# A set's chunks in two goes beside U, and gate weights made one item ahead behind it

## The chip, the cores and the metric

The kernel runs on one core of one Trainium2 chip. The metric is the device time of one execution in microseconds (us); the runs shown are given as a median with the lowest and the highest. A profile is one further execution, recorded instruction by instruction. The engines are PE (matrix multiply; PEld is its loading of stationary operands), DVE (vector), ACT (scalar, activation functions), POOL (here nearly only gathers, that is, indirect DMAs) and SP (which issues plain DMAs). Each runs its own queue in order, and they wait for one another by semaphores.

## What is computed

One layer of a diffusion backbone on 256 latent tokens with 256 context tokens: modulated norm, a combined projection, an mLSTM and a differential attention, gates and an output projection, and then PEER, a retrieval of single-neuron experts. The change lies in PEER and in what follows it. All is float32.

```python
def peer(h, w_pq, sub_keys, expert_u, expert_v):
    ...
    def block(args):
        hx, ix, gx = args
        act = jax.nn.gelu(jnp.einsum('td,ted->te', hx, expert_u[ix]).astype(jnp.float32), approximate=False)
        return jnp.einsum('te,ted->td', (gx * act).astype(h.dtype), expert_v[ix])
...
x = x + g2 * peer(modulate(rmsnorm(x, norm2_w[l]), sh2, sc2), w_pq[l], sub_keys[l], expert_u[l], expert_v[l])
return rmsnorm(x, final_norm_w)
```

Per token and head, ix holds the best 16 of 128 x 128 experts and gx their softmax weights. There are 16384 experts of 2048 numbers in expert_u and in expert_v; each of the 256 tokens takes 128 of them.

## The kernel before

**U.** The kernel computes the product of every token with every row of expert_u. The experts come in 128 columns of 128. A column takes two half blocks of 512 KB: SP loads one (`raw`), ACT casts its high part (`hi`), DVE subtracts to get the low part (`lo`), and PE multiplies both against the tokens (8 matmuls with hi, 8 with lo, tile `s`). Three buffers each of raw, hi and lo let the load run ahead. `u_pair` does two columns; behind each half block `pump` takes steps of the generator `plan`, 1.3 of them on average in the last stretch, so that other work is put between half blocks. GELU goes to `act` and from there to DRAM (`ag_dram`), beside the gates g.

**V.** The output is the sum over experts of gate x activation x row of expert_v. Lists made on the chip say which rows are needed by which 32 tokens. V works on blocks of 128 rows. POOL gathers per block the two factors (`ag`, from ag_dram) and the rows (`vraw`, 1 MB); DVE multiplies the two factors into the block's weights `w`. There are four sorts of blocks. A *set* is four blocks, one for each group of 32 tokens of one 128-token tile; its weights are 32 wide and PE multiplies them with the rows as they are, in four chunks of 512 columns (`v_groups`). `PAIRS` are four blocks that serve a group of 32 in both tiles, in the same manner. *BOTH* and *single* blocks have weights for all 128 tokens of both tiles or of one; here rows and weights are each cut into a high and a low part (`split`: hi and lo, three buffers; `halves`: ACT casts l0, DVE subtracts to l1), and PE makes three products of them, in groups of six matmuls for a half of the columns and one tile (`v_part`). Two *dense* blocks, the last two columns (`N_LIST` = 126 and up), take their weights from `act_tail`, for all 256 tokens at once, into `d`, which has one buffer (`weights_of`, L1571 to L1574).

**Order.** `SOON` are seven sets that `soon()` does beside U, as steps of `plan`. Those of the first tile add up in PSUM (`out_acc[0]`, matmuls that write `v`). The second tile's accumulators are not yet there, so its two sets write each chunk into one of two PSUM buffers `vs`, and ACT copies it (first set, L1670) or DVE adds it (second set, L1668) into `kept`. `multiply` puts all four chunks in one step. Behind U, `out_acc[1]` starts from `kept`, and `ITEMS` follow in order: two sets of the second tile, the two dense blocks, then four rounds of BOTH, single, BOTH, single and so on with a `PAIRS` item in each, and at the end three sets: one of the first tile, two of the second. `v_item(n)` calls `next_item(n)`, which first issues gathers (`fetch`, up to a dozen blocks ahead; twelve rows and twelve `ag` fit), then makes the weights of item n, and then PE's matmuls of item n follow. On DVE the operations marked `line` keep the order in which they are written; PE's and POOL's keep theirs too. ACT's casts and DVE's lo are placed by the scheduler.

**End.** `residual(t, c)` (L1790) multiplies chunk c of a tile with g2 and adds x1 on DVE, and squares it on ACT; `finish_tile(t)` (L1799) sums the squares, takes the root on POOL, scales the four chunks and sends them out. Before the change the order is: set of the first tile; its four residuals; weights and matmuls of the last set but one; weights of the last set; `finish_tile(0)`; the last set's matmuls chunk by chunk, each with its residual; `finish_tile(1)`.

Of the kernel before, what the change touches and what calls it, by code (L numbers as in the profile page):

```python
# [31 lines left out]
P = 128  # L32
D = 2048
T = 256
# [53 lines left out]
def build(tc, a, dump=None):  # L88
# [1475 lines left out]
    def halves(src, n, name, bufs, pool=None):  # L1564
        pool = pool or vst
        r = [pool.tile([P, n], F32R, name=f"{name}{s}", tag=f"{name}{s}", bufs=bufs) for s in range(2)]
        nc.scalar.copy(r[0], src)
        line(nc.vector.tensor_tensor(r[1], src, r[0].bitcast(F32), op=OP.subtract))  # L1568
        return r

    def weights_of(kind, ins):  # L1571
        if kind == DENSE:
            r = halves(act_tail[:, ins - N_LIST, :], T, "d", 1)
            return {t: [x[:, t * P:(t + 1) * P] for x in r] for t in range(2)}  # L1574
        out = {}
        for t, ag in ins.items():
            if kind < 8 or kind >= PAIR:
                g = slice(32 * (group(kind, t) % 2), 32 * (group(kind, t) % 2) + 32)
                out[t] = vst.tile([P, 32], F32, name="w32", tag="w32", bufs=16)
                line(nc.vector.tensor_tensor(out[t], ag[:, 0, 0, g], ag[:, 0, 1, g], op=OP.mult))  # L1580
                continue
            w = vst.tile([P, P], F32, name="w", tag="w", bufs=2)
            line(nc.vector.tensor_tensor(w.rearrange("p (q c) -> p q c", q=2), ag[:, :, 0], ag[:, :, 1], op=OP.mult))  # L1583
            out[t] = halves(w, P, "l", 5)
        return out
# [16 lines left out]
            fetched.append((stage_rows(*BLOCKS_OF[b]), ins))  # L1602
            staged[0] += 1

    def next_item(n):
        fetch(n)
        return [(raw, weights_of(kind, ins)) for (kind, _), (raw, ins) in
                zip(ITEMS[n], [fetched.pop(0) for _ in ITEMS[n]])]

    def accumulators(t):  # L1610
        pool = tc.alloc_tile_pool(name=f"psV{t}", bufs=1, space=PSUM, side=("left", "right")[t], reuse_waits="tile")
# [40 lines left out]
    def soon():  # L1652
        nonlocal psG
        loads = resident()
        psG.release()
        out_acc[0] = accumulators(0)
        work = SOON + ITEMS[:2]
        sums = [0, 0]

        def multiply(item, parts):  # L1660
            t = item[0][0] // 4
            if t == 0:
                v_groups(0, item, parts, first=not sums[0])
            for c in range(4 * t):
                ps = psS.tile([P, 512], F32, name="vs", tag="vs")
                v_groups(1, item, parts, (c,), first=True, last=True, into=ps)
                if sums[1]:
                    line(nc.vector.tensor_tensor(kept[c], ps, kept[c], op=OP.add))  # L1668
                else:
                    nc.scalar.copy(kept[c], ps)  # L1670
            sums[t] += 1

        for n, item in enumerate(work):
            new = []
            if n == 0:
                rows = []
                for b in work[0] + work[1]:
                    rows.append(stage_rows(*b))
                    yield
            for b in item:  # L1680
                while made[0] < columns_of(*b):
                    yield
                new.append(stage_gates(*b))
                yield
            if 0 < n <= len(SOON):
                parts = [(raw, weights_of(kind, ins)) for (kind, _), (raw, ins) in zip(work[n - 1], held)]
            for j, b in enumerate(item):
                new[j] = (stage_rows(*b) if n > 1 else rows.pop(0)), new[j]
                next(loads, None)
                yield  # L1690
            if 0 < n <= len(SOON):
                multiply(work[n - 1], parts)
                yield
            held = new
            if n >= len(SOON):
                fetched.extend(new)
                staged[0] += len(new)
# [3 lines left out]
    for i1 in range(0, P, 2):  # L1701
# [3 lines left out]
        act = act_tail if i1 == N_LIST else gm.tile([P, 2, T], F32, name="act", tag="act", bufs=2)  # L1705
        u_pair(act, pace)
        if i1 == N_LIST:
            parts = next_item(0)
        nc.scalar.activation(act, act, AF.Gelu)
        if i1 < N_LIST:  # L1710
            rows = ag_dram[P + i1 * P:P + (i1 + 2) * P].rearrange("(i p) (t c) -> p i t c", p=P, t=2)
# [22 lines left out]
                v_part(hl, ins[t], t, hf_)  # L1734

    def v_item(n):
        parts = next_item(n)
        if len(parts) > 1:
            for t in parts[0][1]:
                v_groups(t, ITEMS[n], parts)  # L1740
        else:
            v_block(*parts[0])

    for c in range(4):
        mp_(out_acc[1][c], lhsT=ident, rhs=kept[c], start=True, stop=False, skip_group_check=True)
    v_groups(1, ITEMS[0], parts)
    x1[1] = [chunk("x1", "o2") for _ in range(3)] + [kept[3]]
    for c in range(4):
# [66 lines left out]
    fw = [stg.tile([P, 1024], F32, name="fw", tag="raw", bufs=3) for _ in range(2)]  # L1815
    for i in range(2):
        nc.sync.dma_start(fw[i], bass.AP(tensor=fnw.tensor, offset=fnw.offset + i * 1024, ap=[[0, P], [1, 1024]]))
    v_groups(0, ITEMS[N_LAST], next_item(N_LAST), last=True)
    for c in range(4):
        residual(0, c)  # L1820
    last = next_item(N_LAST + 1)
    v_groups(1, ITEMS[N_LAST + 1], last)
    last = next_item(N_LAST + 2)
    finish_tile(0)
    for c in range(4):
        v_groups(1, ITEMS[N_LAST + 2], last, (c,), last=True)
        residual(1, c)
# [72 lines left out]
```

## Time and profile before

| | us |
|---|---|
| median of 3 runs | 2257.23 (2255.82 to 2258.28) |
| profiled execution, its time | 2255.45 |
| profiled execution, its span | 2253.7 |
| PE busy in the span | 2153.0 |
| DVE, ACT, POOL busy | 1533.7, 1021.8, 789.2 |
| last eight matmuls of U start / first set behind U starts | 2025.5 / 2030.2 |
| last set's matmuls end (as modelled) | 2239.0 |

The span is what the trace covers; the time is 1.75 us more. In a row of a timeline the columns are start, length, engine, line, operation, output<-inputs, count, and in brackets the idle time of the engine just before and what ended it. Names are those of the program without buffer numbers: `w` there stands for w and for the 32 wide w32, `l` for l0 and l1, `d` for d0 and d1. A matmul on float32 operands shows as two records, so the 16 matmuls of a set are 32 records. A line can be that of a helper: nearly all matmuls stand at L94, so one reads by tiles.

### The profile page before, as it was taken

How to read it: one execution, taken by the hardware profiler on the slowest of the kernel's cores; microseconds unless marked ns; L12 is line 12 of the kernel's file. 1: busy time of each engine (PE TensorE's matmuls, PEld its weight loads, DVE VectorE, ACT ScalarE, POOL GpSimd, SP SyncE). 2: the span in 40 equal slices, each digit the busy share in tenths (PEclk: the TensorE clock that was granted, in tenths of full speed). 3: DMA queues.
4: the chain of work that ended last, by engine and by line, in shares of the span. 5: the costliest groups of instructions: out<-in, count | busy, mean ns of one | idle time of the engine just before them, and what ended most of it. 6: DMA issues, size and time to landing. Idle time of an engine off the chain costs nothing. (4 is left out here: it accounts for less than half of the span.)

```text
span 2253.7 us, 37192 instructions
## 1 busy us (share of the span) xinstructions
PE 2153.0 (96%) x14098; PEld 1863.2 (83%) x14098; DVE 1533.7 (68%) x2779; ACT 1021.8 (45%) x1632; POOL 789.2 (35%) x799
## 2 busy tenths in 40 slices
PE   6999999999999999998999999998999899999996
PEld 3668998999899999987998888897888776785663
DVE  3438793676986786855679967777999444444655
ACT  3232232224565844444444768873445343333442
POOL 2122210235464320000224657761221423316664
PEclk9999999999999999999999999999999999999998
DMA  9958882776555578875556658888665889989996
GB/s 380 370 172 304 320 295 90 281 254 200 169 160 149 167 266 275 279 254 192 169 169 192 191 172 236 225 225 251 203 196 181 338 311 339 349 286 409 392 357 234
DMA packets 235845, 563.63 MB, mean 250 GB/s; under 512 B 85218, under 2 KB 118803, under 8 KB 222096
## 3 DMA queue, kind: packets, MB, share of 16 engines
q1 hardware_dynamic: 155328, 339.34, 45.8%
q0 software_dynamic: 45488, 204.33, 25.2%
q10 hardware_dynamic: 34848, 17.57, 2.7%
q8 instruction: 111, 1.82, 0.3%
q14 instruction: 70, 0.57, 0.1%
HBM read 516.99 MB, written 38.93 MB: 247 GB/s over the span
## 5 line engine op out<-in xcount | busy, mean ns | idle before, releaser
L140 ACT CAST hi<-raw 128x1024 fp32r<-128x1024 f32 x528 | 553.1, 1049 | 857.5 <-PE acc L300 266.4
L143 DVE TENSOR_TENSOR lo<-raw,hi 128x1024 fp32r<-128x1024 f32 x476 | 599.8, 1263 | 377.7 <-ACT hi L140 341.6
L94 PE MATMUL s<-h,hi 128*128 128x512 f32 x2048 | 528.9, 400 | 13.1 <-ACT hi L140 11.9
L94 PEld LDWEIGHTS s<-h,hi 128*128 128x128 f32 x2048 | 369.9, 190 | 90.9 <-ACT hi L140 16.7
L300 PE MATMUL acc<-hL,hi 128*128 128x256 f32 x2048 | 334.0, 285 | 0.0
L94 PEld LDWEIGHTS s<-h,lo 128*128 128x128 f32 x2048 | 279.4, 190 | 29.7 <-DVE lo L143 5.6
L300 PEld LDWEIGHTS acc<-hL,hi 128*128 128x128 f32 x2048 | 293.3, 192 | 1.8 <-ACT kA L677 0.3
L94 PE MATMUL s<-h,lo 128*128 128x256 f32 x2048 | 286.1, 282 | 6.7 <-DVE lo L143 3.9
L143 POOL TENSOR_TENSOR lo<-raw,hi 128x1024 fp32r<-128x1024 f32 x52 | 133.7, 2572 | 306.9 <-ACT hi L140 243.7
L300 PE MATMUL acc<-hL,lo 128*128 128x256 f32 x1024 | 176.3, 285 | 0.8 <-DVE lo L143 0.8
L533 DVE SCALAR_TENSOR_TENSOR raw<-raw,cr 128x1024 f32<-128x1024 f32 x128 | 155.2, 1227 | 23.6 <-DMA raw<-w_mod 20.2
L118 POOL DMA_DIRECT2D raw<-w_mod x128 | 67.9, 530 | 291.5 <-DVE raw L533 278.0
L1261 POOL TENSOR_SCALAR o<-iota,i1T,gT 128x128 f32<-128x128 f32 x128 | 145.1, 1142 | 58.6 <-PE g L94 29.0
L1532 POOL DMA_INDIRECT vraw<-expert_v,idxV x96 | 101.7, 1060 | 175.5 <-PE v L94 94.2
L300 PEld LDWEIGHTS acc<-hL,lo 128*128 128x128 f32 x1024 | 150.8, 192 | 2.0 <-DVE lo L143 1.0
L1532 POOL DMA_INDIRECT ag<-ag_dram,idxG x96 | 115.6, 1204 | 83.0 <-DMA ag_dram<-act 43.0
L1561 DVE TENSOR_TENSOR lo<-vraw,hi 128x1024 fp32r<-128x1024 f32 x68 | 82.8, 1223 | 83.5 <-ACT hi L1559 82.8
L1244 DVE TENSOR_REDUCE act<-s 128x256 f32<-128x512 f32 x126 | 86.2, 684 | 56.9 <-PE s L94 53.4
L300 PE MATMUL acc<-hC,hi 128*128 128x256 f32 x512 | 124.7, 283 | 0.0
L94 PE MATMUL v<-hi,l 128*128 128x512 f32 x384 | 108.5, 399 | 4.8 <-DVE l L1568 4.6
L1559 ACT CAST hi<-vraw 128x1024 fp32r<-128x1024 f32 x68 | 70.7, 1049 | 91.2 <-PE v L94 89.3
L300 PEld LDWEIGHTS acc<-hC,hi 128*128 128x128 f32 x512 | 98.3, 192 | 0.0
(444 smaller groups left out, 3330.7 us busy)
## 6 DMA issues: line engine op xcount, KB each, us to landing
raw<-expert_u SPq DMA_DIRECT2D x256, 512.0 KB, 4.2
raw<-w_in SPq DMA_DIRECT2D x176, 512.0 KB, 4.5
raw<-w_mod POOLq DMA_DIRECT2D x128, 512.0 KB, 5.3
raw<-w_mod SPq DMA_DIRECT2D x64, 512.0 KB, 8.3
raw<-w_out SPq DMA_DIRECT2D x32, 512.0 KB, 4.3
raw<-w_pq SPq DMA_DIRECT2D x32, 512.0 KB, 3.4
ag_dram<-gates SPq DMA_DIRECT2D x32, 512.0 KB, 6.2
ag_dram<-act ACTq DMA_DIRECT2D x126, 128.0 KB, 4.5
```

The lines of the kernel that those rows point to most:

```text
L94: tc.keep_in_program_order(mm(*args, **kw))
L118: d = queue.dma_start(r, src)
L140: nc.scalar.copy(h, r)
L143: (nc.vector if shared[0] else nc.gpsimd).tensor_tensor(l, r, h.bitcast(F32), op=OP.subtract)
L300: mm(acc[c][:, g * T:(g + 1) * T], lhsT=hl[sb][:, k2 * 512 + c * P:k2 * 512 + (c + 1) * P], rhs=rhs(sa, g, k), start=first and k2 == 0 and ...
L533: product = nc.vector.scalar_tensor_tensor(r, r, 1.0, cr, op0=OP.mult, op1=OP.mult, accum_out=part[:, h, i:i + 1])
L1244: line(nc.vector.reduce_sum(act[:, e], ps.rearrange("p s t -> p t s"), axis=AX.X))
L1261: (nc.gpsimd if i % 2 else nc.vector).tensor_scalar(o2[:, i], iota, cols[:, i:i + 1], factor[:, i:i + 1], op0=OP.is_equal, op1=OP.mult)
L1532: tc.keep_in_program_order(nc.gpsimd.indirect_dma_start(out=out, out_offset=None, in_=src, in_offset=bass.IndirectOffsetOnAxis(ap=idx[:, b ...
L1559: nc.scalar.copy(h, raw)
L1561: nc.vector.tensor_tensor(l, raw, h.bitcast(F32), op=OP.subtract)
```

## The change

It has four parts. `multiply` gives two extra steps behind chunk 1 of a set of the second tile, so that half blocks of U come between its two halves. A dense block's weights are made for each tile apart, in the tag `l` with five buffers in place of `d` with one. `next_item` is split into `fetch` and `item_weights`; behind U, `v_item(n)` fetches, takes the weights made before, and makes those of item n + 1 ahead of its own matmuls. At the end, the weights of the last set but one are made ahead of the first tile's last matmuls, and those of the last set behind that tile's second residual.

```diff
@@ -1570,8 +1570,7 @@
 
     def weights_of(kind, ins):
         if kind == DENSE:
-            r = halves(act_tail[:, ins - N_LIST, :], T, "d", 1)
-            return {t: [x[:, t * P:(t + 1) * P] for x in r] for t in range(2)}
+            return {t: halves(act_tail[:, ins - N_LIST, t * P:(t + 1) * P], P, "l", 5) for t in range(2)}
         out = {}
         for t, ag in ins.items():
             if kind < 8 or kind >= PAIR:
@@ -1602,10 +1601,11 @@
             fetched.append((stage_rows(*BLOCKS_OF[b]), ins))
             staged[0] += 1
 
-    def next_item(n):
-        fetch(n)
+    def item_weights(n):
         return [(raw, weights_of(kind, ins)) for (kind, _), (raw, ins) in
                 zip(ITEMS[n], [fetched.pop(0) for _ in ITEMS[n]])]
+
+    coming = []
 
     def accumulators(t):
         pool = tc.alloc_tile_pool(name=f"psV{t}", bufs=1, space=PSUM, side=("left", "right")[t], reuse_waits="tile")
@@ -1668,7 +1668,11 @@
                     line(nc.vector.tensor_tensor(kept[c], ps, kept[c], op=OP.add))
                 else:
                     nc.scalar.copy(kept[c], ps)
+                if c == 1:
+                    yield
+                    yield
             sums[t] += 1
+            yield
 
         for n, item in enumerate(work):
             new = []
@@ -1689,8 +1693,7 @@
                 next(loads, None)
                 yield
             if 0 < n <= len(SOON):
-                multiply(work[n - 1], parts)
-                yield
+                yield from multiply(work[n - 1], parts)
             held = new
             if n >= len(SOON):
                 fetched.extend(new)
@@ -1705,7 +1708,8 @@
         act = act_tail if i1 == N_LIST else gm.tile([P, 2, T], F32, name="act", tag="act", bufs=2)
         u_pair(act, pace)
         if i1 == N_LIST:
-            parts = next_item(0)
+            fetch(0)
+            parts = item_weights(0)
         nc.scalar.activation(act, act, AF.Gelu)
         if i1 < N_LIST:
             rows = ag_dram[P + i1 * P:P + (i1 + 2) * P].rearrange("(i p) (t c) -> p i t c", p=P, t=2)
@@ -1734,7 +1738,9 @@
                 v_part(hl, ins[t], t, hf_)
 
     def v_item(n):
-        parts = next_item(n)
+        fetch(n)
+        parts = coming.pop()
+        coming.append(item_weights(n + 1))
         if len(parts) > 1:
             for t in parts[0][1]:
                 v_groups(t, ITEMS[n], parts)
@@ -1743,6 +1749,7 @@
 
     for c in range(4):
         mp_(out_acc[1][c], lhsT=ident, rhs=kept[c], start=True, stop=False, skip_group_check=True)
+    coming.append(item_weights(1))
     v_groups(1, ITEMS[0], parts)
     x1[1] = [chunk("x1", "o2") for _ in range(3)] + [kept[3]]
     for c in range(4):
@@ -1815,13 +1822,17 @@
     fw = [stg.tile([P, 1024], F32, name="fw", tag="raw", bufs=3) for _ in range(2)]
     for i in range(2):
         nc.sync.dma_start(fw[i], bass.AP(tensor=fnw.tensor, offset=fnw.offset + i * 1024, ap=[[0, P], [1, 1024]]))
-    v_groups(0, ITEMS[N_LAST], next_item(N_LAST), last=True)
-    for c in range(4):
+    fetch(N_LAST)
+    coming.append(item_weights(N_LAST + 1))
+    v_groups(0, ITEMS[N_LAST], coming.pop(0), last=True)
+    for c in range(2):
         residual(0, c)
-    last = next_item(N_LAST + 1)
-    v_groups(1, ITEMS[N_LAST + 1], last)
-    last = next_item(N_LAST + 2)
+    coming.append(item_weights(N_LAST + 2))
+    for c in range(2, 4):
+        residual(0, c)
+    v_groups(1, ITEMS[N_LAST + 1], coming.pop(0))
     finish_tile(0)
+    last = coming.pop()
     for c in range(4):
         v_groups(1, ITEMS[N_LAST + 2], last, (c,), last=True)
         residual(1, c)
```

On PE, in the second of the two sets beside U. Before, its chunks 1 and 2 (two `vs` buffers, the same four weights):

```order
L94 MATMUL vs_19572<-vraw_19280,w32_19478 32x512
L94 MATMUL vs_19572<-vraw_19280,w32_19480 32x512
L94 MATMUL vs_19572<-vraw_19305,w32_19482 32x512
L94 MATMUL vs_19572<-vraw_19305,w32_19484 32x512
L94 MATMUL vs_19578<-vraw_19280,w32_19478 32x512
L94 MATMUL vs_19578<-vraw_19280,w32_19480 32x512
L94 MATMUL vs_19578<-vraw_19305,w32_19482 32x512
L94 MATMUL vs_19578<-vraw_19305,w32_19484 32x512
```

and after the change, from chunk 1 of the same set on:

```order
L94 MATMUL vs_19594<-vraw_19302,w32_19502 32x512
L94 MATMUL vs_19594<-vraw_19302,w32_19504 32x512
L94 MATMUL vs_19594<-vraw_19355,w32_19506 32x512
L94 MATMUL vs_19594<-vraw_19355,w32_19508 32x512
L94 MATMUL s_19601<-h2_0_10160,hi_19543 128x512
L94 MATMUL s_19601<-h2_1_10161,hi_19543 128x512
L94 MATMUL s_19601<-h2_2_10162,hi_19543 128x512
L94 MATMUL s_19601<-h2_3_10163,hi_19543 128x512
```

Two half blocks of U (32 matmuls) now stand between chunks 1 and 2; the set as a whole comes one half block later in U.

On DVE, in the rounds behind U, around a BOTH block (rows vraw_21519 before, vraw_21543 after) and the single that follows it. Before:

```order
L1583 TENSOR_TENSOR w_21817<-ag_21517 128x128
L1561 TENSOR_TENSOR lo_21831<-vraw_21519,hi_21829 128x1024
L1568 TENSOR_TENSOR l1_21820<-w_21817,l0_21819 128x128
L1583 TENSOR_TENSOR w_21823<-ag_21517 128x128
L1561 TENSOR_TENSOR lo_21847<-vraw_21519,hi_21845 128x1024
L1583 TENSOR_TENSOR w_21861<-ag_21521 128x128
L1561 TENSOR_TENSOR lo_21869<-vraw_21519,hi_21867 128x1024
L1568 TENSOR_TENSOR l1_21826<-w_21823,l0_21825 128x128
L1568 TENSOR_TENSOR l1_21864<-w_21861,l0_21863 128x128
L1561 TENSOR_TENSOR lo_21879<-vraw_21519,hi_21877 128x1024
```

and after:

```order
L1582 TENSOR_TENSOR w_21798<-ag_21541 128x128
L1561 TENSOR_TENSOR lo_21812<-vraw_21462,hi_21810 128x1024
L1568 TENSOR_TENSOR l1_21801<-w_21798,l0_21800 128x128
L1582 TENSOR_TENSOR w_21804<-ag_21541 128x128
L1561 TENSOR_TENSOR lo_21822<-vraw_21462,hi_21820 128x1024
L1582 TENSOR_TENSOR w_21837<-ag_21545 128x128
L1568 TENSOR_TENSOR l1_21807<-w_21804,l0_21806 128x128
L1561 TENSOR_TENSOR lo_21845<-vraw_21543,hi_21843 128x1024
L1568 TENSOR_TENSOR l1_21840<-w_21837,l0_21839 128x128
L1561 TENSOR_TENSOR lo_21861<-vraw_21543,hi_21859 128x1024
```

Before, the low weights of the block's second tile (l1_21826) stand behind three of the lo of the block and the single; after, they (l1_21807) stand ahead of the block's first lo, behind those of the single before it.

On DVE at the end: yf and x are the first tile's residuals, the w32 the weights of the last sets. Before, from the first tile's third residual on:

```order
L1793 TENSOR_TENSOR yf_22520<-v02_18449,g2_2_18910 128x512
L1794 TENSOR_TENSOR x1_18693<-x1_18693,yf_22520 128x512
L1793 TENSOR_TENSOR yf_22524<-v03_18450,g2_3_18912 128x512
L1794 TENSOR_TENSOR x1m_18687<-x1m_18687,yf_22524 128x512
L1580 TENSOR_TENSOR w32_22528<-ag_22312 128x32
L1580 TENSOR_TENSOR w32_22530<-ag_22316 128x32
L1580 TENSOR_TENSOR w32_22532<-ag_22319 128x32
L1580 TENSOR_TENSOR w32_22534<-ag_22323 128x32
L1580 TENSOR_TENSOR w32_22552<-ag_22396 128x32
L1580 TENSOR_TENSOR w32_22554<-ag_22400 128x32
L1580 TENSOR_TENSOR w32_22556<-ag_22481 128x32
L1580 TENSOR_TENSOR w32_22558<-ag_22485 128x32
```

and after, from its second residual on:

```order
L1800 TENSOR_TENSOR yf_22532<-v01_18448,g2_1_18884 128x512
L1801 TENSOR_TENSOR x1_18692<-x1_18692,yf_22532 128x512
L1579 TENSOR_TENSOR w32_22536<-ag_22416 128x32
L1579 TENSOR_TENSOR w32_22538<-ag_22420 128x32
L1579 TENSOR_TENSOR w32_22540<-ag_22497 128x32
L1579 TENSOR_TENSOR w32_22542<-ag_22501 128x32
L1800 TENSOR_TENSOR yf_22544<-v02_18449,g2_2_18910 128x512
L1801 TENSOR_TENSOR x1_18693<-x1_18693,yf_22544 128x512
L1800 TENSOR_TENSOR yf_22548<-v03_18450,g2_3_18912 128x512
L1801 TENSOR_TENSOR x1m_18687<-x1m_18687,yf_22548 128x512
```

The last set's four weights now stand ahead of the first tile's third and fourth residuals; those of the set before it stand ahead of the first residual. The order of POOL's gathers and of SP's loads is the same in both programs.

## The prediction

> **What bounds the kernel now.** I read the page first, then the busy time by stretch, the waits, and last the timelines of the places that the change touches.
>
> ```profile
> PE 2153.0 (96%) x14098; PEld 1863.2 (83%) x14098; DVE 1533.7 (68%) x2779; ACT 1021.8 (45%) x1632; POOL 789.2 (35%) x799
> ```
>
> The matmul queue (PE) is busy for 96% of the span, so a gain can only come from PE's pauses, from matmuls that run slowly, or from the few microseconds behind the last matmul. The change touches nothing before 1840 us. By stretch:
>
> ```profile
> 1840.00:2026.00 186.00, 178.40 (x1065) 140.36 (x1064) 86.83 (x105) 65.40 (x70) 48.80 (x45) 0.98 0.88 325
> 2026.00:2206.00 180.00, 173.70 (x887) 115.12 (x885) 99.72 (x197) 76.98 (x111) 118.39 (x104) 0.99 0.96 380
> 2040.00:2110.00 70.00, 66.34 (x305) 47.37 (x304) 38.90 (x76) 30.34 (x44) 49.55 (x45) 0.98 1.02 412
> ```
>
> Columns are the stretch, its length, busy time of PE, weight loads, DVE, ACT, POOL, granted clock, DMA share, GB/s. PE lacks 7.6 us of 186 while U still runs, and 6.3 us of 180 behind it. DVE, ACT and POOL have room on average, so a PE pause is a matter of order, not of load. The transfers are another thing: 412 GB/s at a share of 1.02 for 70 us is all they do anywhere. The waits of PE from 1700 us on (total, times, longest):
>
> ```profile
> PE s L94 <- ACT hi L140: 7.5, 6, 3.5
> PE v L94 <- DVE l L1568: 4.6, 11, 0.7
> PE vs L94 <- DVE kept L1668: 4.5, 1, 4.5
> ```
>
> The first is U waiting for its own input; the change only moves when that can happen. The other two are pauses that it goes for.
>
> **Part 1: the second tile's sets beside U in two goes.** PE's timeline around both sets (start, length, idle before and its releaser):
>
> ```profile
> 1844.53 1.92 PE L94 MATMUL vs<-vraw,w 128*32 128x512 f32 x16
> 1847.27 1.06 PE L94 MATMUL vs<-vraw,w 128*32 128x512 f32 x8 [0.82 <-ACT kept L1670]
> 1849.56 1.06 PE L94 MATMUL vs<-vraw,w 128*32 128x512 f32 x8 [1.23 <-ACT kept L1670]
> 1850.56 2.11 PE L94 MATMUL s<-h,hi 128*128 128x512 f32 x8
> ...
> 1870.31 3.64 PE L94 MATMUL v<-vraw,w 128*32 128x512 f32 x32
> 1873.88 2.14 PE L94 MATMUL s<-h,hi 128*128 128x512 f32 x8
> ...
> 1876.79 2.00 PE L94 MATMUL s<-h,hi 128*128 128x512 f32 x8
> ...
> 1893.64 1.92 PE L94 MATMUL vs<-vraw,w 128*32 128x512 f32 x16
> 1900.10 3.64 PE L94 MATMUL vs<-vraw,w 128*32 128x512 f32 x16 [4.54 <-DVE kept L1668]
> 1903.67 3.01 PE L94 MATMUL s<-h,hi 128*128 128x512 f32 x8
> ...
> 1907.46 2.00 PE L94 MATMUL s<-h,hi 128*128 128x512 f32 x8
> ```
>
> A set of the first tile, which waits for nothing, takes 1873.88 - 1870.31 = 3.57 us, and a half block of U behind it 1876.79 - 1873.88 = 2.91. The first of the two sets takes 1850.56 - 1844.53 = 6.03, so 2.46 too much. The second with its half block takes 1907.46 - 1893.64 = 13.82 against 3.57 + 2.91 = 6.48, so 7.34 too much: 4.54 of waiting, and slow matmuls behind it (16 in 3.64 where 1.92 do, 8 in 3.01 where 2.14 do). With two half blocks of U between the goes, the two copies (ACT) or additions (DVE) that chunks 2 and 3 wait for have some 5.8 us. Both stalls go: 9.8. What is late next is U's input, because the pause had covered it:
>
> ```profile
> 1893.23 1.05 ACT L140 CAST hi<-raw 128x1024 fp32r<-128x1024 f32 x1 [4.41 <-DMA raw<-expert_u]
> ```
>
> This half is ready at 1894.28, and the second set now comes one half block later, so PE wants it at 1893.64 and waits 0.6. I take 9.2. The lower end is one wait of the longest kind above (3.5) on top: 5.7; the upper 9.8. The four more steps (1.3 per half block) push the loads of the last early set some three half blocks back; POOL's gathers then rest until U ends, so that costs nothing:
>
> ```profile
> 2024.11 0.95 POOL L1532 DMA_INDIRECT ag<-ag_dram,idxG  x1 [43.02 <-DMA ag_dram<-act]
> ```
>
> **Part 2: dense weights in five buffers.** Behind U, PE multiplies two dense blocks, in eight groups of six:
>
> ```profile
> 2040.09 1.09 PE L94 MATMUL v<-hi,d 128*128 128x512 f32 x4
> ...
> 2041.49 1.09 PE L94 MATMUL v<-hi,d 128*128 128x512 f32 x4
> ...
> 2044.23 0.73 PE L94 MATMUL v<-hi,d 128*128 128x512 f32 x2 [1.18 <-ACT d L1567]
> 2045.72 1.22 PE L94 MATMUL v<-hi,d 128*128 128x512 f32 x2 [0.76 <-DVE d L1568]
> ...
> 2052.74 1.17 PE L94 MATMUL v<-hi,l 128*128 128x512 f32 x4
> ```
>
> A group takes 2041.49 - 2040.09 = 1.40. The last five should take 7.0 and take 2052.74 - 2041.49 = 11.25: 4.25 lost, because the one buffer d makes the second block's weights wait for the first block's matmuls. With the weights of both blocks made at U's end this goes, but for some 0.3 at the step to the first listed block, where no d is waited for: 3.9. The four smaller casts and subtractions replace two larger ones while PE still multiplies the sets in front. Lower end: the waiting alone, 1.18 + 0.76 = 1.9. The other 2.3 are matmuls at about half pace (1.22 for two, where two take 0.62 in part 3's rows). The Trainium skill, "TensorE: Matmul & The Clock Gate" (Part 1: The HAM clock gate, the "warmup" mystery), lets the clock drop only after an idle window of about 3.4 us; by that rule these pauses would cost no clock and the sum would be 2.0 smaller, but in this trace pauses of 1.18 and 0.76 did bring slow matmuls, and the measurement decides.
>
> **Part 3: weights one item ahead.** Of the eleven waits for l, one:
>
> ```profile
> 2146.74 1.09 PE L94 MATMUL v<-hi,l 128*128 128x512 f32 x4
> ...
> 2148.14 0.62 PE L94 MATMUL v<-hi,l 128*128 128x512 f32 x2
> 2149.16 0.73 PE L94 MATMUL v<-hi,l 128*128 128x512 f32 x2 [0.40 <-DVE l L1568]
> ...
> 2150.20 1.09 PE L94 MATMUL v<-hi,l 128*128 128x512 f32 x4
> ```
>
> A group takes 2148.14 - 2146.74 = 1.40, this one 2150.20 - 2148.14 = 2.06: 0.66 lost. The order shows why: DVE makes the second tile's low weights two lo behind their w. Now they stand ahead of the block's own first lo, and w, cast and l of an item are all queued while PE still multiplies the one before. The same DVE and ACT work is done, only sooner. The queue that it moves past holds hi and lo; DVE is busy 99.72 of 180 us there, so a lo that starts two short operations later stays ahead of PE. Ten of the eleven come before 2206 us: 10 x 0.66, and 0.3 for the longest (0.7): 6.9. If the low weights come only half as much sooner, 3.4. PE's gain moves the time at which the buffers of the last group of four come free.
>
> **Part 4: the last weights nearer the front.** From there on POOL's gathers set the pace:
>
> ```profile
> 2206.29 0.94 POOL L1532 DMA_INDIRECT vraw<-expert_v,idxV  x1 [5.72 <-PE v L94]
> ...
> 2224.86 0.94 POOL L1532 DMA_INDIRECT ag<-ag_dram,idxG  x1 [0.31 <-issue]
> ```
>
> ```profile
> 2216.85 0.73 PE L94 MATMUL v<-hi,l 128*128 128x512 f32 x2 [0.39 <-DVE l L1568]
> 2230.35 8.67 PE L94 MATMUL v<-vraw,w 128*32 128x512 f32 x64 [3.13 <-DVE w L1580]
> ```
>
> ```profile
> 2227.46 0.68 DVE L1793 TENSOR_TENSOR yf<-v,g 128x512 f32<-128x512 f32 x1
> ...
> 2229.51 0.69 DVE L1794 TENSOR_TENSOR x1m<-x1m,yf 128x512 f32<-128x512 f32 x1
> ...
> 2231.18 0.19 DVE L1580 TENSOR_TENSOR w<-ag 128x32 f32<-128x32 f32 x1 [0.27 <-DMA ag<-ag_dram,idxG]
> 2231.29 0.15 DVE L1800 TENSOR_REDUCE s<-s 128x1 f32<-128x4 f32 x1
> ...
> 2234.33 0.74 DVE L1809 SCALAR_TENSOR_TENSOR x<-x,rf,fw 128x512 f32<-128x512 f32 x1
> 2236.49 0.69 DVE L1793 TENSOR_TENSOR yf<-v,g 128x512 f32<-128x512 f32 x1 [1.42 <-PE v L94]
> ```
>
> PE's pause of 3.13 goes, but the end does not come sooner. POOL starts this chain when the last group of four is done and then waits for nothing, so the last gates land at the same distance from that point: 2231.18 on the old clock. DVE now asks for them after two residuals instead of four. Queued behind that wait are residuals 2 and 3 of the first tile, its sum, its four scalings, and all of the second tile's end. So the third residual starts at 2231.3, the fourth's addition 2229.51 - 2227.46 = 2.05 later, the sum 2231.29 - 2229.51 = 1.78 after that (ACT squares in between), and the scalings end 2234.33 + 0.74 - 2231.29 = 3.78 later: 2238.9. The second tile's first residual, which started at 2236.49, starts there: 2.4 later. PE's sooner matmuls are no help, since the residuals then follow each other on DVE as they do now. Bounds: 0 if the gates land before DVE asks, and up with their landing time:
>
> ```profile
> DMA to landing us min/median/max: 4.7/8.2/11.7
> ```
>
> The last took 2231.18 - 2224.86 = 6.3; at 11.7 the end loses 2.4 + 5.4 = 7.8.
>
> **The sum.** 9.2 + 3.9 + 6.9 - 2.4 = 17.6 us less. The profiled execution took 2255.45 us (span 2253.7), 1.8 under the median of the runs, 2257.23; it becomes 2237.9, and the median 2239.6, 0.8% less. A difference under 0.2% (4.5 us) counts as none here.
>
> **The rivals.**
>
> *The transfers hold the stretch behind U.* There 180 us x 380 GB/s = 68.4 MB move; at 412 that takes 166 us, so the 10.8 us of parts 2 and 3 just fit under the 14 that the transfers allow. If they give no more than today's mean, only part 1 and the end are left: -9.2 + 2.4 = -6.8, 2250.4 us. For it: the share of 0.96. Against: the 412 held for 70 us, and gathers issued a dozen blocks ahead. The Trainium skill, "DMA: Bandwidth & Descriptors" (Where 436 GB/s comes from), names about 358 GB/s as a core's limit on reads from HBM; by that rule this rival would hold; the trace has more over 70 us and decides. Chance 0.10.
>
> *The low weights stay late*, because ACT's casts of weights queue behind casts of blocks that wait for PE: part 3 gives nothing, -9.2 - 3.9 + 2.4 = -10.7, 2246.5 us. The order speaks against it. Chance 0.09.
>
> *The end loses nothing*, if the last gates land 4 us sooner, with fewer transfers around them: -20.0, 2237.2 us. Chance 0.11.
>
> *Slower: the gathers set the pace in both stretches.* Place: the gather queue from 1840 us on. PE's saved pauses then turn into waits for rows, the last group of four ends when it does now, and only part 4 is left: +2.4, 2259.6 us, with gates that land as now, to +7.8, 2265.0 us, at the longest landing. It decides once the DMA share stays at 1.0 throughout; beside U it is 0.88. Chance 0.10, half within 0.2%, half beyond.
>
> **How the numbers follow.** The forecast has 0.60. The range, 2235.5 to 2250.5, takes in its bounds (2236.3 with 9.8, 4.2 and nothing lost at the end, 2248.6 with 5.7, 1.9 and 3.4), about a microsecond of scatter, and the first three rivals; the slower one and what lies beyond the bounds stay out. Faster 0.60 + 0.10 + 0.09 + 0.11 = 0.90; the last rival splits into 0.05 and 0.05.
>
> **What would show it.** Right: no vs wait for kept, v<-hi,l groups 1.40 apart throughout, no wait for dense weights; at the end a DVE wait of 3 to 4 us for ag ahead of the third residual, and the second tile's first residual bound by DVE, not by PE. Wrong: casts that wait for vraw behind U (first rival), l still the releaser of PE (second), no ag wait on DVE (third), or group-of-four ends that have not moved (fourth).

## The result and the profile after

The changed kernel takes 2240.06 us (median of 6 runs, 2236.07 to 2244.98), the kernel before 2256.63 on the same chip (6 runs, 2255.82 to 2258.28): a ratio of 0.9932, 95% interval 0.9913 to 0.9952. The profiled execution of the changed kernel took 2240.84 us (span 2239.1), that of before 2255.45.

I split both traces at three places that every version of the kernel has. V is the first `vs` matmul (U's second half), K the first matmul `v<-kept,ident` (U's end), G the start of the last group of four (`v<-vraw,w` x64, 7.07 us long). The rows of the changed kernel, PE's timeline:

```profile
1844.01 1.92 PE L94 MATMUL vs<-vraw,w 128*32 128x512 f32 x16
...
1851.64 1.92 PE L94 MATMUL vs<-vraw,w 128*32 128x512 f32 x16
...
1894.30 1.92 PE L94 MATMUL vs<-vraw,w 128*32 128x512 f32 x16
...
1901.93 1.92 PE L94 MATMUL vs<-vraw,w 128*32 128x512 f32 x16
...
2020.47 2.93 PE L94 MATMUL v<-kept,ident 128*128 128x512 f32 x6
...
2182.17 7.07 PE L94 MATMUL v<-vraw,w 128*32 128x512 f32 x64
...
2206.16 8.15 PE L94 MATMUL v<-vraw,w 128*32 128x512 f32 x70
2217.05 3.59 PE L94 MATMUL v<-vraw,w 128*32 128x512 f32 x26 [2.73 <-DMA vraw<-expert_v,idxV]
```

Before, V, K and G stood at 1844.53, 2026.46 and 2198.92. So the 14.6 us between the two spans are: 0.5 ahead of V, where nothing was changed; 181.93 - 176.46 = 5.5 beside U; 172.46 - 161.70 = 10.8 behind it; and 56.93 - 54.78 = 2.2 lost at the end. The four goes of `vs` have no wait any more. All of PE's waits from 1700 us on, and the busy time by stretch:

```profile
PE s L94 <- ACT hi L140: 8.9, 8, 3.0
PE v L94 <- DMA vraw<-expert_v,idxV: 2.7, 1, 2.7
```

```profile
1840.00:2019.00 179.00, 176.41 (x1056) 139.86 (x1055) 86.19 (x105) 65.02 (x70) 49.51 (x45) 0.99 0.90 334
2019.00:2185.00 166.00, 165.85 (x855) 114.82 (x858) 101.38 (x200) 77.66 (x114) 114.42 (x104) 1.00 1.01 408
```

The waits for kept, d, l and w are gone; what is left is U's input and one wait for rows at the very end. Behind U PE is busy for 165.85 of 166 us, and the transfers have 408 GB/s on average. The last five dense groups and the step behind them, which took 11.25 us before, take 2042.81 - 2035.50 = 7.31:

```profile
2035.50 1.10 PE L94 MATMUL v<-hi,l 128*128 128x512 f32 x4
...
2042.81 1.17 PE L94 MATMUL v<-hi,l 128*128 128x512 f32 x4
```

Beside U a part was given back. Here are PE's timeline, POOL's some 20 us earlier, and ACT's just ahead of PE's wait:

```profile
1993.61 1.11 PE L94 MATMUL s<-h,lo 128*128 128x256 f32 x8
1996.47 2.85 PE L94 MATMUL s<-h,hi 128*128 128x512 f32 x8 [1.75 <-ACT hi L140]
1999.12 1.91 PE L94 MATMUL s<-h,lo 128*128 128x256 f32 x8
```

```profile
1974.87 1.23 POOL L1532 DMA_INDIRECT vraw<-expert_v,idxV  x1 [12.48 <-PE v L94]
1976.40 0.94 POOL L1532 DMA_INDIRECT vraw<-expert_v,idxV  x1 [0.30 <-issue]
1977.64 0.96 POOL L1532 DMA_INDIRECT vraw<-expert_v,idxV  x1 [0.30 <-PE s L94]
1978.90 1.43 POOL L1532 DMA_INDIRECT vraw<-expert_v,idxV  x1 [0.30 <-issue]
```

```profile
1990.56 1.05 ACT L140 CAST hi<-raw 128x1024 fp32r<-128x1024 f32 x1 [2.17 <-DMA raw<-expert_u]
1995.37 1.04 ACT L140 CAST hi<-raw 128x1024 fp32r<-128x1024 f32 x1 [3.76 <-DMA raw<-expert_u]
```

A set's buffers come free all at once, POOL asks for its four megabytes within 5.5 us, and behind that U's own loads (`raw`) arrive late, so ACT's cast and PE wait. Whether the one makes the other is a question for the runs with spaced gathers. The end, on DVE:

```profile
2210.72 0.19 DVE L1579 TENSOR_TENSOR w<-ag 128x32 f32<-128x32 f32 x1 [0.40 <-DMA ag<-ag_dram,idxG]
2214.52 0.19 DVE L1579 TENSOR_TENSOR w<-ag 128x32 f32<-128x32 f32 x1 [3.61 <-DMA ag<-ag_dram,idxG]
2214.63 0.68 DVE L1800 TENSOR_TENSOR yf<-v,g 128x512 f32<-128x512 f32 x1
...
2221.25 0.75 DVE L1816 SCALAR_TENSOR_TENSOR x<-x,rf,fw 128x512 f32<-128x512 f32 x1
2221.91 0.68 DVE L1800 TENSOR_TENSOR yf<-v,g 128x512 f32<-128x512 f32 x1
```

DVE stands 3.61 us at the last gates; the first tile's third residual starts only then (2214.63), and the second tile's first residual follows the scalings without a wait for PE.

### The profile page after: what moved, and what is told of

Its sections match the earlier page's. It is cut to its first block, busy times and chain, and to the rows that moved or that the text cites. A ratio compares the mean times of both kernels' runs of the same rounds, so it can differ in the third digit from the quotient of the medians.

```text
span 2239.1 us, 37163 instructions
## 1 busy us (share of the span) xinstructions
PE 2146.8 (96%) x14098; PEld 1860.9 (83%) x14098; DVE 1536.1 (69%) x2781; ACT 1022.1 (46%) x1634; POOL 784.5 (35%) x799
## 5 line engine op out<-in xcount | busy, mean ns | idle before, releaser
L300 PE MATMUL acc<-hL,lo 128*128 128x256 f32 x1024 | 175.7, 284 | 0.9 <-DVE lo L143 0.9
L1261 POOL TENSOR_SCALAR o<-iota,i1T,gT 128x128 f32<-128x128 f32 x128 | 147.5, 1160 | 56.4 <-PE g L94 27.9
L1532 POOL DMA_INDIRECT vraw<-expert_v,idxV x96 | 101.5, 1057 | 167.5 <-PE v L94 83.5
L1532 POOL DMA_INDIRECT ag<-ag_dram,idxG x96 | 109.9, 1145 | 79.7 <-DMA ag_dram<-act 37.4
L94 PE MATMUL v<-hi,l 128*128 128x512 f32 x416 | 114.5, 397 | 0.1
```

The costliest lines, as they stand in the source:

```text
L94: tc.keep_in_program_order(mm(*args, **kw))
L300: mm(acc[c][:, g * T:(g + 1) * T], lhsT=hl[sb][:, k2 * 512 + c * P:k2 * 512 + (c + 1) * P], rhs=rhs(sa, g, k), start=first and k2 == 0 and ...
L1261: (nc.gpsimd if i % 2 else nc.vector).tensor_scalar(o2[:, i], iota, cols[:, i:i + 1], factor[:, i:i + 1], op0=OP.is_equal, op1=OP.mult)
L1532: tc.keep_in_program_order(nc.gpsimd.indirect_dma_start(out=out, out_offset=None, in_=src, in_offset=bass.IndirectOffsetOnAxis(ap=idx[:, b ...
```

## The experiments

My theory: part 1 takes away stalls and hands some of it back as late input for U; parts 2 and 3 give what was predicted; part 4 costs, because DVE's queue stands at the last gates. The rivals stand in each expectation. Three later comparisons, each of four kernels on one chip with its own runs of the kernel before, are called chips two to four; chip one is that of the result. The table has the marks of all traces. It is the key to what follows: V, ahead of which PE's work is the same in all kernels, lies anywhere between 1844.0 and 1855.4, so totals of single executions mean little, but stretches between marks can be compared. A ratio is taken over all runs of both kernels and need not be that of the medians; where the text turns one into microseconds, it is that share of the median of before.

| chip, trace | sets beside U | V to K | K to G | G to the end | timed against before, 95% interval |
|---|---|---|---|---|---|
| one: before | one go | 181.9 | 172.5 | 54.8 | |
| one: changed | two goes | 176.5 | 161.7 | 56.9 | 0.9932 (0.9913 to 0.9952) |
| two: e1 | two goes | 174.2 | 172.3 | 55.1 | 0.9982 (0.9968 to 0.9996) |
| two: e2 | one go | 178.2 | 161.7 | 55.6 | 0.9945 (0.9928 to 0.9963) |
| two: e3 | one go | 178.3 | 172.6 | 55.9 | 1.0012 (1.0001 to 1.0024) |
| two: e6 | one go | 178.7 | 168.3 | 55.2 | 0.9986 (0.9974 to 0.9998) |
| three: e0, changed | two goes | 174.2 | 170.9 | 55.9 | 0.9953 (0.9938 to 0.9968) |
| three: e4 | two goes | 174.8 | 181.7 | 58.5 | 0.9956 (0.9942 to 0.9971) |
| three: e5 | spaced | 172.3 | 173.7 | 57.2 | 0.9947 (0.9928 to 0.9966) |
| three: e7 | spaced | 171.6 | 175.8 | 58.1 | 0.9957 (0.9938 to 0.9975) |
| four: e8 | spaced | 173.6 | 174.0 | 56.9 | 0.9956 (0.9937 to 0.9975) |
| four: e9 | two goes | 173.2 | 167.5 | 56.5 | 0.9965 (0.9948 to 0.9982) |
| four: e10 | two goes | 174.3 | 169.3 | 55.5 | 0.9951 (0.9933 to 0.9969) |
| four: e11, before | one go | 175.7 | 172.7 | 56.6 | one run |

The medians of the kernel before were 2254.85 on chip two (29 runs, 2249.07 to 2261.49), 2263.35 on three and 2257.22 on four.

**Part 1 alone (e1).** The diff's hunks in `multiply` and behind it, nothing else.

> The kernel before with part 1 alone: the second tile's sets beside U in two goes. Theory (the stalls go, but U's own loads are late behind bursts of gathered rows, which gives part of it back): 5.5 us less than before, about 2251.1; no wait of vs for kept, but U's matmuls wait 2 to 3 us in all for their input hi, the longest near 1996 us. Rival (what the prediction said: 9.8 of stalls less one wait of 0.6): 9.2 less, about 2247.4, and what the changed kernel lacks of that was lost behind U. On the scatter: if the changed kernel's 9 us between its fastest and slowest run come from U's late loads, this kernel scatters as widely; if they come from behind U, it stays within the 2.5 us of the kernel before.

It took 2252.03 us (12 runs); 0.18% of 2254.85 is 4.1 us (0.9 to 7.2). The stretch V to K says the same: 178.6 on average over the five traces with one go, 174.5 over the six with two, 4.0 less. No wait of `vs` for kept is left. 9.2 is out, while the timing alone leaves room for 5.5. Taken chip by chip the difference in V to K is 5.5 on chip one, 4.2 on two and 2.0 on four, so its size is uncertain by some 2 us. U waits 1.9 us for hi, but the longest wait, 0.83, is near 1950 and not near 1996. On the scatter both ideas fell: before itself spreads over 12.4 us on this chip, so a spread of 9 us does not need the change (on chip one, in six runs, before had 2.5).

**Parts 2 and 3 without 1 and 4 (e2).** The changed kernel with `multiply` (its lines are left out here) and the end as before:

```
     fetch(N_LAST)
-    coming.append(item_weights(N_LAST + 1))
     v_groups(0, ITEMS[N_LAST], coming.pop(0), last=True)
-    for c in range(2):
-        residual(0, c)
-    coming.append(item_weights(N_LAST + 2))
-    for c in range(2, 4):
+    for c in range(4):
         residual(0, c)
+    coming.append(item_weights(N_LAST + 1))
     v_groups(1, ITEMS[N_LAST + 1], coming.pop(0))
+    coming.append(item_weights(N_LAST + 2))
     finish_tile(0)
```

> The kernel before with parts 2 and 3 alone (dense weights in five buffers, an item's weights made one item ahead), the sets beside U in one go and the end in its old order. Theory: 10.8 less than before, about 2245.8, groups of six 1.40 apart behind U. Rival (the transfers hold that stretch, and part 1 paid for it by letting the gathers behind U start sooner): clearly less than 10.8, with PE or ACT's casts waiting for gathered rows. On the scatter: narrow like the kernel before if U's loads make it, wide if the stretch behind U does.

2243.23 us (6 runs), 0.55% or 12.4 less (8.3 to 16.2), and K to G in 161.7: the rival that needed part 1 for this falls. PE's waits behind U are down to the one at the end, as before.

**The new end alone (e3).** Before, with the last lines of the diff.

> The kernel before with part 4 alone: the last weights nearer the front, nothing else changed. Theory (DVE stands 3 to 4 us at the last gates, with two residuals, a sum and four scalings queued behind): 2.2 us more, about 2258.8, and the second tile's first residual starts about 2.2 later than at 2236.49 without waiting for PE. Rival (PE's pause of 3.13 us before the last set was on the path): 3 us less, about 2253.5.

2258.59 us (12 runs), 0.12% more, that is 2.7 us (0.2 to 5.4). The rival, a gain of 3, is out. In its trace DVE waits less than in the changed kernel, and G to the end is 0.3 to 1.1 us longer than in the four traces of chips one and two with the old end:

```profile
2231.97 0.19 DVE L1580 TENSOR_TENSOR w<-ag 128x32 f32<-128x32 f32 x1 [2.39 <-DMA ag<-ag_dram,idxG]
2232.08 0.68 DVE L1794 TENSOR_TENSOR yf<-v,g 128x512 f32<-128x512 f32 x1
```

On chips one and two the two new ends average 56.4, the four old ones 55.2: 1.3 us. The traces of chips three and four, taken later, do not bear this out: two new ends of 55.9 and 57.2, four old ones of 55.5 to 56.9, 56.6 and 56.4 on average. Waits that the first two chips do not show lie in these ends as well (e0 has one of 2.55 us on DVE, of the kind described at the end of this section). So the loss rests on chips one and two and on the timing of e3, whose interval begins close to nothing (0.2 us).

**Dense weights alone (e6).** Before, with the two lines of `weights_of`.

> The kernel before with part 2 alone: the dense blocks' weights for each tile apart, in five buffers. Theory: the 4.25 us that the last five dense groups lose go but for 0.3, so 3.9 less, about 2252.7; the half-pace matmuls behind the pauses go with the pauses. Rival one (only the waiting itself goes, the matmuls stay slow): 1.9 less, about 2254.7. Rival two (the step to the first listed block takes the time back, since its weights are then the late ones): no change.

2252.50 us (12 runs), 0.14% or 3.2 less (0.5 to 5.9); K to G is 4.1 shorter, where the four traces with the old stretch lie within 0.4 of each other. Both rivals name values inside or near the interval of the timing, so the trace decides, against both.

**The changed kernel on another chip (e0), and the end turned further back (e4).**

> The changed kernel once more, beside the next three on one chip. Theory: 2240 us, with a scatter of several us from run to run, because the moment at which U's loads fall behind the bursts of gathered rows is not the same each time. Rival: the wide scatter was that of one chip, and here the runs lie within 2.5 us.

2251.27 us (12 runs) where before has 2263.35: the ratio holds within the intervals, the times do not. They spread over 12 us, and before's over 17 on this chip, so the rival on the scatter falls, and the theory's reason, which is of the changed kernel alone, does not explain it. All four kernels of chip three have K to G 9 to 20 us longer than 161.7; more below. e4 is:

```
-    for c in range(2):
-        residual(0, c)
-    coming.append(item_weights(N_LAST + 2))
-    for c in range(2, 4):
+    for c in range(4):
         residual(0, c)
     v_groups(1, ITEMS[N_LAST + 1], coming.pop(0))
     finish_tile(0)
+    coming.append(item_weights(N_LAST + 2))
```

> The changed kernel with the last set's weights behind the first tile's four residuals, sum and scalings, and all else as changed. Theory (DVE's wait for the last gates holds up what is queued behind it): the wait of 3 to 4 us stands there no more, the second tile's first residual starts near 2218.3 instead of 2221.9, and the end comes 3.4 us sooner than in the changed kernel, about 2236.6. Rival (PE's last matmuls, which then wait for the weights made later, hold the residuals): no gain, or up to 2 us more.

No gain (2253.32), and G to the end is 58.5, where e0 has 55.9. DVE's and PE's rows show that the rival was right:

```profile
2243.20 0.75 DVE L1816 SCALAR_TENSOR_TENSOR x<-x,rf,fw 128x512 f32<-128x512 f32 x1
2243.86 0.49 DVE L1579 TENSOR_TENSOR w<-ag 128x32 f32<-128x32 f32 x4
2246.38 0.69 DVE L1800 TENSOR_TENSOR yf<-v,g 128x512 f32<-128x512 f32 x1 [2.03 <-PE v L94]
```

```profile
2244.10 6.32 PE L94 MATMUL v<-vraw,w 128*32 128x512 f32 x32 [6.12 <-DVE w L1579]
```

The gates have landed by then, but now the weights wait for the scalings, PE 6.12 us for the weights, and DVE's next residual 2.03 for PE. Of the three places this is the worst (58.5, and 58.1 in e7). Between the other two, the old one, between the residuals and the sum, is ahead by the 1.3 us of chips one and two, and level on three and four.

**Spaced gathers (e5, e7).** Behind each of 24 gathers of rows beside U, those of six sets, two short operations on POOL; the last set's four gathers ahead of U's end stay as they were. The lines that set up the counter and the tile `rest` are left out:

```
             gather(raw, FULL, idxV, BASE[kind] + i)
+            gathered[0] += 1
+            if 8 < gathered[0] <= 32:
+                for _ in range(2):
+                    tc.keep_in_program_order(nc.gpsimd.tensor_scalar(rest[0], iota, iota[:, 1:2],
+                        iota[:, 2:3], op0=OP.is_equal, op1=OP.mult))
```

> The changed kernel with a rest of two short operations (128x128, some 1.2 us each) on POOL behind each of the 24 gathers of rows beside U from the third set on, so that four megabytes are asked for over some 16 us and not over 5. Theory (U's loads are late because they queue with bursts of four gathers): U's waits for hi of 2 to 3 us and the slow matmuls behind them go, 3 to 4 us less than the changed kernel, about 2236.5, and the runs lie closer together. Rival (U's loads are late for another reason, say the amount moved in all): no change, 2240 us, the same waits and scatter. Rival two (the rows now come too late for the sets beside U): slower, with v or vs waiting for vraw.

> Both together: the rests between the gathers beside U, and the last set's weights behind the first tile's end. The two lie at different places, so each theory expects its own gains to add: by mine about 7 us less than the changed kernel, some 2233; if only the end's order is right, 2236.6; if only the spacing, 2236.5.

Timed they are level with e0 (2251.54 and 2253.21). In the stretch itself the effect shows; from V to K, the busy times of e7, where PE does not wait once, and of e0:

```profile
1847.23:2018.78 171.55, 171.55 (x1042) 136.18 (x1042) 85.85 (x102) 64.53 (x69) 95.78 (x85) 1.00 0.92 340
```

```profile
1846.14:2020.29 174.15, 172.35 (x1041) 136.40 (x1041) 83.84 (x102) 64.06 (x69) 52.82 (x45) 1.00 0.90 334
```

As many bytes move, only less bunched, and U's waits for hi fall from 1.7 to nothing (0.8 in e5, 1.5 in e8). The waits that are left speak for the theory too: in all three traces PE waits for nothing as long as the gathers are spaced, and the one wait of e5 and that of e8 come at 1999.60 and 1991.38, some 16 to 20 us behind the four gathers that were not spaced (from 1979.33 and 1975.74). In e7 the same unspaced four (from 1976.82) make PE wait for nothing, so a burst can make U's input late but need not. What it is worth is less sure: 174.5 against 172.5 on average, 2.5 less on chip three, but nothing on chip four (173.6 against 173.2 and 174.3). I had expected 3 to 4.

**Old end with and without spacing, a shorter queue, and before again (e8 to e11).** e9 is the changed kernel with the end of e2; e8 adds the rests of e5; e10 changes in e9's `fetch` the number 11 into 7 (and fetches ahead of the last two items); e11 is the kernel before.

> The kernel before once more, for its trace beside the next three on one chip. Theory (how long the sets beside U stall differs from one execution to the next, and the profiled execution of before had the long case): first vs to the end of U takes near 178.4 us, as in the three other kernels with the old sets, and not 181.9; the wait for kept that was 4.54 is shorter. Rival (that execution was typical): 181.9. Behind U: 172.5 us from U's end to the last group of four where the engines do not stand still, 8 to 20 more where they do; if this chip shows them, the old kernel shows them as well.

> The changed kernel with the end in its old order and with the rests of two short operations behind each gather of rows beside U. By my marks: 172.0 us from the first vs to U's end (two goes, spaced), 161.7 from there to the last group of four, 55.2 for the rest: 7.3 + 10.8 less than before with 179.3 and 172.5, that is 18 us or 0.8%, where the engines do not stand still behind U. Rival (spacing gives back behind U what it gains beside it): no better than the next kernel.

> The changed kernel with the end in its old order alone. Theory: 174.4 beside U, 161.7 behind it, 55.2 for the rest, so 15.7 us less than before (0.7%) and 1.3 less than the changed kernel (56.5 at its end). Rival (the new end is worth as much as the old where the weights are made early): the same as the changed kernel.

> The kernel with the old end, and gathers behind U issued at most eight blocks ahead instead of twelve. Two theories on the 8 to 20 us in which ACT, DVE and PE stood still behind U on one chip while gathers went on. One: they wait for something that queues with a dozen gathers, so a shorter queue takes most of it away, and the time from U's end to the last group of four comes near 162 us on any chip. Other: the queue has nothing to do with it; they stand as long, and where they do not stand, the shorter run-ahead costs up to 5 us with waits for rows.

e11 has 175.7 from V to K and a wait for kept of 2.95: the profiled execution of before was the long case, and 178.4 was still too much here. Behind U it has 172.7, as on chip one, while the three new kernels there have 167.5 to 174.0 and not 161.7. So on this chip the new stretch suffers more, though the old one is made up otherwise too. Its dense pauses are the same as on chip one, but the matmuls behind them run at full pace:

```profile
2039.97 0.73 PE L94 MATMUL v<-hi,d 128*128 128x512 f32 x2 [1.18 <-ACT d L1567]
2041.46 0.73 PE L94 MATMUL v<-hi,d 128*128 128x512 f32 x2 [0.76 <-DVE d L1568]
2042.03 0.63 PE L94 MATMUL v<-lo,d 128*128 128x512 f32 x2
```

The last five dense groups therefore take 10.07 us, 1.2 less than the 11.25 to 11.32 of before, e1 and e3, and waits for lo (1.2) and longer ones for l (up to 1.2) take that back. The medians of e8, e9 and e10 (2247.07, 2248.76, 2248.55) tell no version from another, and none from the changed kernel's ratio. The shorter queue takes nothing away: 169.3 against 167.5, in one trace each.

So 18 and 15.7 us less were expected of e8 and e9, and some 10 and 8 came, because K to G did not come down to 161.7 there. (e8's traced execution took 2252.47 us, 5 above its median, so its 174.0 may be one of the longer stretches.) What the engines do in the lost time, in the worst trace (e4, the slowest of its 12 runs), by tens of microseconds, and who they wait for between 2066 and 2100:

```profile
2060.00:2070.00 10.00, 10.00 (x73) 4.98 (x75) 6.82 (x16) 4.32 (x8) 4.87 (x6) 1.00 1.03 416
2070.00:2080.00 10.00, 8.66 (x46) 5.82 (x38) 0.00 (x0) 0.00 (x0) 7.56 (x9) 1.00 1.01 411
2080.00:2090.00 10.00, 3.29 (x6) 1.66 (x6) 1.42 (x2) 1.04 (x1) 7.36 (x8) 0.60 1.02 416
2090.00:2100.00 10.00, 4.79 (x13) 3.85 (x14) 4.30 (x7) 3.81 (x6) 1.54 (x2) 0.55 0.99 404
```

```profile
ACT hi L1559 <- remote: 24.9, 2, 13.3
DVE lo L1561 <- remote: 15.8, 1, 15.8
...
PE v L94 <- ACT hi L1559: 8.4, 1, 8.4
```

DVE and ACT do nothing for 10 us, then PE follows, while POOL goes on issuing gathers and the transfers run at their full 411 to 416 GB/s. "Remote" stands for a releaser that the view does not find. ACT's two waits:

```profile
2081.46 1.04 ACT L1559 CAST hi<-vraw 128x1024 fp32r<-128x1024 f32 x1 [13.28 <-remote]
2094.11 1.04 ACT L1559 CAST hi<-vraw 128x1024 fp32r<-128x1024 f32 x1 [11.60 <-remote]
```

The trace does hold the semaphore events, and by them what ends both waits is PE, whose matmuls signal that a buffer has been read. PE's signals of that time stand at 2081.39, at 2084.20 (DVE's lo starts at 2084.29), and then six of them from 2094.04 to 2094.29. But the last matmul with a signal had ended at 2078.66 for the first two and at 2086.79 for the six, so they are at least 2.7, 5.5 and 7.2 us late. From K to G, in the six traces of chips one and two every signal of PE comes within 0.11 us of the end of its matmul. In the seven new traces of chips three and four 24 to 38 of them are more than 0.25 us late, the longest by 3.1 to 12.1; in e11 it is 8, the longest by 1.7. The signals of ACT and DVE that are on record are late in none. So late rows are not what ACT waited for in the first place, nor in e7's longest wait (9.55 us, ended by PE's signal at 2082.26, the rows' own standing at 2074.55); in the second place above a landing stands at 2092.55, so rows may have part in it. Why PE's signals are late is open. The traces of chips three and four also lack records (of some 110 signals of ACT in the stretch they have 72 to 80), so that the recording itself takes part can't be excluded.

In all seven new traces on chips three and four PE also loses 0.8 to 3.2 us 23 to 25 us behind K, put down to its sequencer at the branch ahead of the rounds (L1767, L1775 in the spaced kernels), where the changed kernel on chip one loses 0.3. Why two chips do this and two do not stays open; on chips one and two a single trace each (changed, e2) has the whole new stretch.

## Why the prediction was right, and where it was not

The median came out at 2240.06 against 2239.6, and the direction and most of the size were right. Of the terms:

- **Parts 2 and 3** (3.9 and 6.9): right in size and place on chips one and two. The dense weights alone give 4.1 (e6), both together 10.8 (changed kernel, e2), with no wait for d or l left. The price of the dense pauses was one execution's, too: of the 3.9, some 2 were slow matmuls behind pauses of 1.18 and 0.76 us, which before, e1 and e3 have and e11 has not. On chips three and four the waits for d and l go as well, but other waits take 6 to 20 us of the stretch.
- **Part 1** (9.2): mis-sized, and by the step that priced it from one execution. The mechanism is right, both stalls go. But the second set's stall differs from one execution to the next. From the second set's first `vs` to U's next matmul it took 10.03 us in the profile of before and 7.62, 9.09, 7.23 and 6.72 in e2, e3, e6 and e11, where 3.57 do. PE's timelines of e2 and e6, and the busy times of the two stretches behind the waits:

```profile
1898.57 3.58 PE L94 MATMUL vs<-vraw,w 128*32 128x512 f32 x16 [2.18 <-DVE kept L1668]
```

```profile
1898.00:1902.00 4.00, 3.43 (x16) 0.59 (x16) 2.94 (x4) 0.33 (x1) 0.00 (x0) 0.57 0.86 236
```

```profile
1901.93 1.92 PE L94 MATMUL vs<-vraw,w 128*32 128x512 f32 x16 [3.44 <-DVE kept L1667]
```

```profile
1900.00:1904.00 4.00, 2.07 (x17) 0.63 (x18) 3.95 (x5) 1.59 (x3) 0.00 (x0) 1.00 0.80 263
```

  The wait varies, and whether the slow matmuls follow varies too. Before's execution had the longest wait and the slow matmuls. The first set's stall varies as well: its go takes 6.03 us in before and 4.59 to 5.15 in the other four. On average the part gives 4.0, below the 5.7 that I had set as its lower bound. The late input of U, taken at 0.6, is the small part of the error, some 0.5 of 5.2 us: waits for hi are 2.1 on average with two goes and 1.0 with one.
- **Part 4** (2.4 lost): right in mechanism, DVE's wait and the order behind it are as forecast. The size is less sure: 2.2 in the two profiles compared, 1.3 on average over chips one and two, 2.7 timed (0.2 to 5.4), 0.2 on three and four. DVE's wait is 3.61 us in the changed kernel and 2.39 in e3, and follows when the last gates land.
- **The rivals.** The transfers did not hold the stretch: 408 GB/s over 166 us on chip one. The Trainium skill, "DMA: Bandwidth & Descriptors" (Where 436 GB/s comes from), would have had them stop at about 358; no trace here shows that limit. On chips three and four the stretch does lose 6 to 20 us, in e4 at a full DMA share, which resembles that rival; but the longest waits of ACT in e4 and e7 (13.28 and 9.55 us) ended with late signals of PE, and not with rows. The low weights are not late, the end does lose on chips one and two, and nothing made the kernel slower.

So the total came out so close partly by luck. The two profiled executions differ by 14.6 us and not by the 17.6 of the sum, and 5.5 of that is part 1 as single executions on chip one show it; the medians, 2257.23 in the forecast and 2240.06, happen to lie 17.2 apart. By the averages the sum is 4.0 + 10.8 - 1.3 = 13.5 us or 0.6%, which the ratios 0.9932 and 0.9953 bracket; it holds where the stretch behind U takes its 161.7 us.

## What to carry to other kernels

A stall in one profile is one draw: before pricing its removal, look at the same stretch in a second execution, and compare stretches between marks rather than whole spans. Work that is only made earlier on idle engines pays in full when the operands' buffers are there and nothing else holds the stretch (10.8 us on two of four chips here). Asking for something earlier on an in-order queue pays nothing if it has not landed, and it delays all that stands behind; asking too late makes others wait: of three places for the same four small multiplies the last one was the worst, and the first no better than the one between.

## What the runs showed of the hardware

- The length of a pause alone does not tell the granted clock behind it. In e2 it is 0.57 behind a wait of 2.18 us, in e6 it stays at 1.00 behind 3.44 (rows above); pauses of 1.18 and 0.76 us bring slow matmuls in three traces and none in e11. The Trainium skill, "TensorE: Matmul & The Clock Gate" (Part 1: The HAM clock gate), asks for an idle window of about 3.4 us; the first of these cases has less and drops.
- Transfers ran at 408 GB/s on average over 166 us. Behind a burst of four gathers of 1 MB, asked for within 5.5 us, 512 KB loads on another queue came late: a cast that needed one waited 3.76 us, though in e7 such a burst cost PE nothing.
- On two chips PE's semaphore signals came up to 12 us behind the matmul's end, in bunches (six within 0.25 us), while ACT's and DVE's came in time; on the two others none was more than 0.11 us late.
- One program's time differs by chip: the kernel before has medians from 2254.85 to 2263.35, the changed one 2240.06 and 2251.27, with the same matmuls.
